# Order edges on TensorE, ScalarE and VectorE, compressed q behind the neighbourhood groups, latent v and k ahead of q, probabilities scaled on VectorE

## The chip, the cores and the metric

The kernel runs on one core of a Trainium2 chip. The metric is device time in microseconds (us), taken from outside the profile. The kernel before takes 1472.89 us, the median of three runs (1472.82 to 1473.05). The kernel multiplies fp32 numbers as pairs of fp32r halves, so TensorE does three products for each one of the reference.

## The reference

One encoder layer on x of 256 tokens by 2048 features, with 256 memory tokens:

```python
h = rmsnorm(x); z = h @ w_in                 # q, k, v (8 heads x 128), c_q (512), c_kv (256), k_rope (64)
A = neighbourhood_attention(q, k, v, rpb)    # softmax(q k' / sqrt(128) + bias) v on a 4 x 64 grid
q2 = rmsnorm(c_q) @ w_uq                     # 8 heads x (128 + 64 rotary)
k2, v2 = split(rmsnorm(c_kv) @ w_ukv)        # 8 heads x (128 + 128)
B = softmax((q2 k2' + rope(q2r) rope(k_rope)') / sqrt(192)) v2
x = x + concat(rmsnorm(A), rmsnorm(B)) @ w_out
x = x + memory_attention(rmsnorm(x), rmsnorm(mem))   # 4 heads of 512
x = x + (silu(n @ w_gate) * (n @ w_up)) @ w_down     # n = rmsnorm(x), d_ff = 5632
out = rmsnorm(x)
```

## The kernel before

**Weights.** All weights stand in one array in the order of their use, as 496 pieces of 128x1024 numbers. SP's queue loads two pieces a transfer into three buffers (`raw`). `split` (L105 to L113) makes two halves of a piece: ScalarE copies it into fp32r (`whi`, L108), then VectorE subtracts that copy (`wlo`, L109). Where a scale is given, the same is L111 on ScalarE and L112 on VectorE. There are three buffers for split pieces, and `piece` (L152) calls for splits two pieces ahead (one ahead for the first 16).

**Products.** `linear` (L225) walks over the 128-row blocks k of a weight and for each does six products of 512 columns on TensorE, three for each half of the tokens (L221 to L223: hi by hi, hi by lo, lo by hi). A full piece is 12 such products. The result gathers in a PSUM buffer `pm` (128x1024); the pool `psm` has two of them. All smaller PSUM tiles (`pt`, `ps`, `py`, `pv`) come from the four buffers of the pool `psa`. A group of latent q or k uses `mm_block` (L186) in place of L221 to L223, and `combine` (L241) adds its two parts: ScalarE copies one (`cmt`, L244), VectorE adds the other (`cmu`, L246). The name of a tile carries a number in the order of the program.

**Background.** Everything beside the products is written as jobs, generators that yield a number of ticks (`Background`, L161). `linear` ticks twice after each k, and a job goes on when its ticks are used up; so the W_ numbers say where in the stream of products the transposes, scores and softmax steps of a head are written. `na_head` (L505) is a head of neighbourhood attention: turn q and k (L303), split, scores, `softmax_steps` (L352: maximum, exponentials, reciprocal, and the scaling of the probabilities on ScalarE at L370), turn the probabilities, values (`head_out`, L498). `compressed` (L464) takes the sums of squares of c_q or c_kv (L253), their rstd (VectorE, POOL, VectorE), evacuates (`ct`, L296), turns it and splits it into `cs`. `rope_job` (L541), `q_job` (L554), `k_job` (L561) and `mla_project` (L567) make latent q, k and the rotary part; `load_mem` (L627) brings the memory's tokens (`mraw`, `mtok`), both in one buffer.

**Order.** Before, the written order is only a priority: a scheduler with a cost model moves an instruction ahead of another on its engine where it holds that to be ready sooner. The projections run as v, c_q, c_kv, four groups q and k of two heads each, the rotary part, q 0, k 0 and 1, q 1, v, then the output projection with the second half of q and k inside it.

```python
        bg.add(rope_job(linear(cs, 4)))
        mla_project(0)
        for i in range(2):
            split_v(linear(cs[:, 4:6], 2), vy_ml[:, 4 * i:4 * i + 4])
```

Of the kernel before, what the change touches and what calls it, by code (L numbers as in the profile page):

```python
# [19 lines left out]
P = 128  # L20
# [31 lines left out]
W_TR = 4  # L52
W_QK, W_EXP, W_PT, W_PV = 4, 3, 5, 6
W_HEADS = 8
W_RS = 5
# [5 lines left out]
def tile_hybrid_encoder(ctx, tc, x, xt, mem, memt, gains, fgain, rope, rpb, weights, out):  # L61
# [9 lines left out]
    psa = ctx.enter_context(tc.tile_pool(name="psa", bufs=4, space=PSUM))  # L71

# [32 lines left out]
    def split(dst_hi, dst_lo, src, scale=None):  # L105

        if scale is None:
            nc.scalar.activation(dst_hi, src, AF.Copy)  # L108
            nc.vector.tensor_sub(dst_lo, src, dst_hi.bitcast(F32))  # L109
        else:  # L110
            nc.scalar.activation(dst_hi, src, AF.Copy, scale=scale)  # L111
            nc.vector.scalar_tensor_tensor(dst_lo, src, scale, dst_hi.bitcast(F32),  # L112
                                           op0=OP.mult, op1=OP.subtract)  # L113
# [72 lines left out]
    def mm_block(ps, whi, wlo, a, first, last):  # L186

        rhs = a.rearrange("p s t -> p (s t)")
        if last and not first:
            nc.tensor.matmul(ps[:, 0:T], wlo, a[:, 0, :], start=False, stop=False)  # L190
            nc.tensor.matmul(ps, whi, rhs, start=False, stop=True)
        else:
            nc.tensor.matmul(ps, whi, rhs, start=first, stop=False)  # L193
            nc.tensor.matmul(ps[:, 0:T], wlo, a[:, 0, :], start=False, stop=last)

    def mm_split(ps, a, b, first, last):

        for i, (u, v) in enumerate(((0, 0), (0, 1), (1, 0))):
            nc.tensor.matmul(ps, a[:, u, :], b[:, v, :], start=first and i == 0, stop=last and i == 2)  # L199
# [18 lines left out]
    def products(o, ak, t, hi, lo, first, last):  # L218

        ts_ = slice(t * P, (t + 1) * P)  # L220
        nc.tensor.matmul(o, ak[:, 0, ts_], hi, start=first, stop=False)  # L221
        nc.tensor.matmul(o, ak[:, 0, ts_], lo, start=False, stop=False)  # L222
        nc.tensor.matmul(o, ak[:, 1, ts_], hi, start=False, stop=last)  # L223

    def linear(a, nk, pm=None, ks=None, cw=CW):  # L225
# [4 lines left out]
        for k in ks or range(nk):  # L230
            if k % per == 0:
# [6 lines left out]
            bg.tick(2)  # L238
        return pm

    def combine(pm):  # L241

        t = scr.tile([P, 2, T], F32, name="cmt", tag="sq")
        nc.scalar.activation(t, pm[:, :, T:2 * T], AF.Copy)  # L244
        dst = scr.tile([P, 2, T], F32, name="cmu", tag="pr", bufs=3)
        nc.vector.tensor_add(dst, pm[:, :, 0:T], t)  # L246
# [3 lines left out]
    def sumsq(dst, src, scale=1.0):  # L250

        junk = scr.tile([P, CW], F32, name="junk", tag="sq")
        nc.scalar.activation(junk[:, :src.shape[-1]], src, AF.Square, scale=scale, accum_out=dst)  # L253

    def square_into(acc, src, first):
        if first:
            nc.scalar.activation(acc, src, AF.Square)
        else:
            q = scr.tile([P, 2, T], F32, name="sq", tag="sq")[:, :src.shape[1]]
            nc.scalar.activation(q, src, AF.Square)  # L260
            nc.gpsimd.tensor_tensor(acc, acc, q, op=OP.add)

    def rstd_of(sums, d, name):

        ms = const.tile([P, TT], F32, name=f"ms_{name}")
        nc.vector.tensor_scalar(ms, sums, 1.0 / d, EPS, op0=OP.mult, op1=OP.add)
# [4 lines left out]
    def rstd_parts(parts, d, name):  # L271

        sums = const.tile([P, TT], F32, name=f"su_{name}")
        nc.vector.tensor_reduce(sums, parts, axis=AX.X, op=OP.add)
        return rstd_of(sums, d, name)

    def rstd_col(acc, n, d, name):

        pc = psa.tile([P, 2 * T], F32, name="pc", tag="a")
        for t in range(TT):  # L280
            for j in range(n):
                nc.tensor.matmul(pc[:, t:t + 1], acc[:, j, t * P:(t + 1) * P], ones[:, 0:1],
                                 start=j == 0, stop=j == n - 1)
# [4 lines left out]
    def rstd_job(acc, n, d, name, wait=1):  # L288
        yield wait
# [3 lines left out]
    def evacuate(pm, dst, rc, w=CW):  # L293

        for t in range(TT):
            nc.scalar.activation(dst[:, t, :], pm[:, t, 0:w], AF.Copy, scale=rc[:, t:t + 1])  # L296

    def turn(src, f0, nf=2):

        pt = psa.tile([P, 2, T], F32, name="pt", tag="a")  # L300
        for f in range(nf):
            for t in range(TT):
                nc.tensor.transpose(pt[:, f, t * P:(t + 1) * P], src[:, t, (f0 + f) * P:(f0 + f + 1) * P], ident)  # L303
# [17 lines left out]
    def residual_job(pm, g, rc=None, parts=None, nxt=None, g0=None, name=None):  # L321


        cs_ = slice(g * CW, (g + 1) * CW)
        for t in range(TT):
            if rc is None:
                nc.vector.tensor_add(xr[:, t, cs_], xr[:, t, cs_], pm[:, t, :])
            else:
                nc.vector.scalar_tensor_tensor(xr[:, t, cs_], pm[:, t, :], rcs[rc][:, t:t + 1], xr[:, t, cs_],
                                               op0=OP.mult, op1=OP.add)  # L330
# [527 lines left out]
```

## Time and profile before

| | us |
|---|---|
| median of three runs | 1472.89 |
| the profiled execution | 1472.88 |
| its span (first to last instruction) | 1471.1 |
| TensorE busy | 1453.7 (99%) |
| VectorE busy | 794.0 (54%) |
| ScalarE busy | 720.1 (49%) |
| GpSimd busy | 22.1 (2%) |

The profiled execution is 1.8 us longer than its span. The HBM traffic is 187 GB/s over the span. The mean granted clock of TensorE is 0.996 of full speed. In the rows, PE is TensorE's products, PEld its weight loads (which run beside products), DVE VectorE, ACT ScalarE, POOL GpSimd and SP the queue that issues transfers. A product's record lasts longer than the distance to the next one's start, since products overlap.

### The profile page before, as it was taken

How to read it: one execution, taken by the hardware profiler on the slowest of the kernel's cores; microseconds unless marked ns; L12 is line 12 of the kernel's file. 1: busy time of each engine (PE TensorE's matmuls, PEld its weight loads, DVE VectorE, ACT ScalarE, POOL GpSimd, SP SyncE). 2: the span in 40 equal slices, each digit the busy share in tenths (PEclk: the TensorE clock that was granted, in tenths of full speed). 3: DMA queues.
4: the chain of work that ended last, by engine and by line, in shares of the span. 5: the costliest groups of instructions: out<-in, count | busy, mean ns of one | idle time of the engine just before them, and what ended most of it. 6: DMA issues, size and time to landing. Idle time of an engine off the chain costs nothing.

```text
span 1471.1 us, 16942 instructions
## 1 busy us (share of the span) xinstructions
PE 1453.7 (99%) x6812; PEld 1212.7 (82%) x6812; DVE 794.0 (54%) x874; ACT 720.1 (49%) x982; POOL 22.1 (2%) x39
## 2 busy tenths in 40 slices
PE   9999999999999999999999999999999999999997
PEld 7878888888888888888888888888888888888886
DVE  5565687667454454545545555445454445555554
ACT  6455677656544554445444444444333444444443
POOL 0000000100000000000000000000000000000000
PEclk9999999999999999999999999999999999999999
DMA  9865444365755444545555555555555555555553
GB/s 356 257 189 172 144 143 144 129 225 198 249 201 172 165 150 166 178 159 184 189 183 199 178 196 195 180 197 180 193 199 198 186 188 194 180 197 193 180 199 115
DMA packets 48718, 275.90 MB, mean 188 GB/s; under 512 B 12992, under 2 KB 13120, under 8 KB 16576
## 3 DMA queue, kind: packets, MB, share of 16 engines
q1 hardware_dynamic: 48064, 273.47, 54.7%
q8 instruction: 53, 0.87, 0.3%
q10 hardware_dynamic: 576, 1.36, 0.3%
q14 instruction: 25, 0.20, 0.0%
HBM read 272.71 MB, written 3.05 MB: 187 GB/s over the span
## 4 chain that ended last, share of the span: by engine, by line
PE 95%; DMA 2%; ACT 1%; DVE 1%; issue 1%; POOL 0%; DVEq 0%; ACTq 0%; POOLq 0%
PE pm L222 28%; PE pm L223 28%; PE pm L221 28%; PE pt L303 2%; PE ps L199 2%; PE py L199 2%; DMA mtok<-in_memt 1%; PE pv L221 1%; PE pv L222 1%; PE pv L223 1%; PE pl L223 0%; PE pl L222 0%; PE pl L221 0%; PE pm L193 0%; ACT whi L108 0%
## 5 line engine op out<-in xcount | busy, mean ns | idle before, releaser
L109 DVE TENSOR_TENSOR wlo<-raw,whi 128x1024 fp32r<-128x1024 f32 (+1 forms) x493 | 602.2, 1223 | 601.9 <-ACT whi L108 601.5
L108 ACT ACTIVATE whi<-raw 128x1024 fp32r<-128x1024 f32 (+1 forms) x493 | 520.8, 1058 | 580.9 <-PE pm L223 565.2
L221 PE MATMUL pm<-whi,x3s 128*128 128x512 f32 x704 | 275.7, 392 | 0.0
L223 PE MATMUL pm<-whi,x3s 128*128 128x512 f32 x704 | 274.1, 389 | 0.0
L222 PE MATMUL pm<-wlo,x3s 128*128 128x512 f32 x704 | 274.0, 389 | 0.0
L223 PEld LDWEIGHTS pm<-whi,x3s 128*128 128x128 f32 x704 | 132.1, 188 | 27.5
L222 PEld LDWEIGHTS pm<-wlo,x3s 128*128 128x128 f32 x704 | 132.2, 188 | 27.0
L221 PEld LDWEIGHTS pm<-whi,x3s 128*128 128x128 f32 x704 | 132.2, 188 | 26.8
L221 PE MATMUL pm<-whi,ms 128*128 128x512 f32 x256 | 101.7, 397 | 0.0
L223 PE MATMUL pm<-whi,ms 128*128 128x512 f32 x256 | 99.9, 390 | 0.0
L222 PE MATMUL pm<-wlo,ms 128*128 128x512 f32 x256 | 99.9, 390 | 0.0
L221 PE MATMUL pm<-whi,ha 128*128 128x512 f32 x224 | 87.5, 391 | 0.0
L223 PE MATMUL pm<-whi,ha 128*128 128x512 f32 x224 | 87.2, 389 | 0.0
L222 PE MATMUL pm<-wlo,ha 128*128 128x512 f32 x224 | 87.2, 389 | 0.0
L221 PE MATMUL pm<-whi,xs 128*128 128x512 f32 (+1 forms) x192 | 74.6, 389 | 0.3 <-ACT whi L108 0.3
L222 PE MATMUL pm<-wlo,xs 128*128 128x512 f32 (+1 forms) x192 | 73.5, 383 | 0.4 <-DVE wlo L109 0.2
L223 PE MATMUL pm<-whi,xs 128*128 128x512 f32 (+1 forms) x192 | 73.2, 381 | 0.0
L223 PEld LDWEIGHTS pm<-whi,ms 128*128 128x128 f32 x256 | 48.1, 188 | 10.4
L222 PEld LDWEIGHTS pm<-wlo,ms 128*128 128x128 f32 x256 | 48.2, 188 | 8.8
L221 PEld LDWEIGHTS pm<-whi,ms 128*128 128x128 f32 x256 | 48.2, 188 | 8.8
L221 PE MATMUL pm<-whi,x2s 128*128 128x512 f32 x128 | 50.1, 391 | 0.8 <-ACT whi L108 0.8
L222 PE MATMUL pm<-wlo,x2s 128*128 128x512 f32 x128 | 49.9, 390 | 0.8 <-DVE wlo L109 0.8
(247 smaller groups left out, 1912.0 us busy)
## 6 DMA issues: line engine op xcount, KB each, us to landing
raw<-in_weights SPq DMA_DIRECT2D x247, 1024.0 KB, 4.9
xr<-in_xt SPq DMA_DIRECT2D x2, 1024.0 KB, 10.7
bias<-skew SPq DMA_DIRECT2D x16, 128.0 KB, 6.4
mraw<-in_mem SPq DMA_DIRECT2D x4, 512.0 KB, 4.8
mtok<-in_memt SPq DMA_DIRECT2D x4, 512.0 KB, 5.1
xf<-in_x SPq DMA_DIRECT2D x7, 256.0 KB, 8.0
fg<-in_fgain SPq DMA_DIRECT2D x1, 1024.0 KB, 7.4
out<-xr SPq DMA_DIRECT2D x2, 512.0 KB, 3.8
```

What stands on the lines that cost most here:

```text
L108: nc.scalar.activation(dst_hi, src, AF.Copy)
L109: nc.vector.tensor_sub(dst_lo, src, dst_hi.bitcast(F32))
L199: nc.tensor.matmul(ps, a[:, u, :], b[:, v, :], start=first and i == 0, stop=last and i == 2)
L221: nc.tensor.matmul(o, ak[:, 0, ts_], hi, start=first, stop=False)
L222: nc.tensor.matmul(o, ak[:, 0, ts_], lo, start=False, stop=False)
L223: nc.tensor.matmul(o, ak[:, 1, ts_], hi, start=False, stop=last)
L303: nc.tensor.transpose(pt[:, f, t * P:(t + 1) * P], src[:, t, (f0 + f) * P:(f0 + f + 1) * P], ident)
```

## The change

Five things change.

1. **Order edges.** `ordered = tc.keep_in_program_order` is put around nearly every instruction of TensorE, ScalarE and VectorE. On each of these engines the instructions then run as they are written. Instructions of POOL and transfers are not wrapped.
2. **Job order and ticks.** Compressed q is projected behind the four neighbourhood groups; compressed kv comes right behind v. The tick numbers change (W_TR, W_QK, W_EXP, W_PT, a W_ROPE of 9, 12 ticks between the two heads of a group), and a narrow k step ticks once.
3. **Latent order.** Behind compressed q come v 0, k 0 and 1, v 1, k 2 and 3, the rotary part, q 0 and q 1; q 2 and q 3 stand in the output projection. The weight array is built in the new order. The jobs of rstd and residual wait until their heads are done.
4. **Scaling.** `softmax_steps` scales the probabilities with VectorE's `tensor_scalar_mul`, not with ScalarE's activation.
5. **Small moves.** The sums of squares of x come one step later; `mtok` has the two buffers of the tag `gate`; the buffer of `qr` lies in another pool.

```diff
--- before.py
+++ after.py
-W_TR = 4
-W_QK, W_EXP, W_PT, W_PV = 4, 3, 5, 6
+W_TR = 5
+W_QK, W_EXP, W_PT, W_PV = 6, 2, 8, 6
 W_HEADS = 8
-W_RS = 5
+W_ROPE = 9
+    ordered = tc.keep_in_program_order
...
         if scale is None:
-            nc.scalar.activation(dst_hi, src, AF.Copy)
-            nc.vector.tensor_sub(dst_lo, src, dst_hi.bitcast(F32))
+            ordered(nc.scalar.activation(dst_hi, src, AF.Copy))
+            ordered(nc.vector.tensor_sub(dst_lo, src, dst_hi.bitcast(F32)))
...
-            bg.tick(2)
+            bg.tick(2 if cw == CW else 1)
...
-    def rstd_job(acc, n, d, name, wait=1):
-        yield wait
+    def rstd_job(acc, n, d, name, ready):
+        while not ready():
+            yield 1
+        yield W_TR
...
         for t in range(TT):
-            nc.scalar.activation(pr[:, t, :], pr[:, t, :], AF.Copy, scale=rs[:, t:t + 1])
+            ordered(nc.vector.tensor_scalar_mul(pr[:, t, :], pr[:, t, :], rs[:, t:t + 1]))
...
-            if j in (5, 6):
+            if j in (6, 7):
...
-        bg.add(compressed(linear(xs, KB), RANK_Q, "q", 0, 4))
         bg.add(compressed(linear(xs, KB, cw=KVR), RANK_KV, "kv", 4, 2))
...
-                bg.add(na_head(2 * i + j, qt, W_TR + (14 if i < NAH // 2 - 1 else 2) * j))
+                bg.add(na_head(2 * i + j, qt, W_TR + 12 * j))
+        bg.add(compressed(linear(xs, KB), RANK_Q, "q", 0, 4))
...
+        def project_v(i):
+            split_v(linear(cs[:, 4:6], 2), vy_ml[:, 4 * i:4 * i + 4])
...
+        project_v(0)
+        project_k(0)
+        project_v(1)
+        project_k(2)
         bg.add(rope_job(linear(cs, 4)))
-        mla_project(0)
-        for i in range(2):
-            split_v(linear(cs[:, 4:6], 2), vy_ml[:, 4 * i:4 * i + 4])
+        project_q(0)
         bg.add(mla_heads())
-        bg.add(rstd_job(acc_na, 1, NAH * P, "na", 2))
+        project_q(1)
+        bg.add(rstd_job(acc_na, 1, NAH * P, "na", lambda: done[G_NA] == NAH))
         for g in range(DM // CW):
             if g == 1:
-                mla_project(2)
-            bg.add(residual_job(linear(vy_na, NAH), g, rc="na"))
+                project_q(2)
+                project_q(3)
+            bg.add(residual_job(linear(vy_na, NAH, ready=lambda: done[G_NA]), g, rc="na"))
...
-                r = hp.tile([P, TT, CW], F32, name="mtok", tag="mraw", bufs=1)
+                r = scr.tile([P, TT, CW], F32, name="mtok", tag="gate")
```

`project_q` and `project_k` are the two halves of `mla_project`, unchanged inside.

**Place A: TensorE, the turn of compressed kv.** `pm_668` gathers c_kv, `ct_880` is its evacuation, `kr_910` its rotary key, `pm_839` the first neighbourhood group. Before, behind c_kv's last products (320 columns):

```order
L221 MATMUL pm_668<-whi_772,xs_78 128x320
L222 MATMUL pm_668<-wlo_773,xs_78 128x320
L223 MATMUL pm_668<-whi_772,xs_78 128x320
L303 MATMUL pt_901<-ident_89,ct_880 128x128 x4
L303 MATMUL pt_939<-ident_89,kr_910 128x128
L221 MATMUL pm_839<-whi_797,xs_78 128x512
L303 MATMUL pt_939<-ident_89,kr_910 128x128
L222 MATMUL pm_839<-wlo_798,xs_78 128x512
L223 MATMUL pm_839<-whi_797,xs_78 128x512
L221 MATMUL pm_839<-whi_797,xs_78 128x512
```

After, `ct_699` is c_kv's evacuation and `pm_654` the first neighbourhood group:

```order
L224 MATMUL pm_654<-whi_683,xs_78 128x512
L225 MATMUL pm_654<-wlo_684,xs_78 128x512
L226 MATMUL pm_654<-whi_683,xs_78 128x512
L309 MATMUL pt_734<-ident_89,ct_699 128x128 x4
L224 MATMUL pm_654<-whi_683,xs_78 128x512
L225 MATMUL pm_654<-wlo_684,xs_78 128x512
L226 MATMUL pm_654<-whi_683,xs_78 128x512
L224 MATMUL pm_654<-whi_683,xs_78 128x512
```

The four transposes of `ct` moved from directly behind c_kv's last product into the middle of the fourth weight piece of the next group, and the rotary key's moved further behind.

**Place B: ScalarE behind v.** `pv_139` to `pv_142` are the sums of v, `vy_na_128` where they go. Before:

```order
L108 ACTIVATE whi_458<-raw_408 128x1024
L108 ACTIVATE whi_478<-raw_456 128x1024
L111 ACTIVATE vy_na_128<-pv_139,rc_x_498 128x4x128
L111 ACTIVATE vy_na_128<-pv_140,rc_x_498 128x4x128
L108 ACTIVATE whi_511<-raw_456 128x1024
L111 ACTIVATE vy_na_128<-pv_141,rc_x_498 128x4x128
L111 ACTIVATE vy_na_128<-pv_142,rc_x_498 128x4x128
L108 ACTIVATE whi_517<-raw_474 128x1024
```

After (`pa_x_143` are the sums of squares of x, in front of v's evacuations):

```order
L257 ACTIVATE junk_492,pa_x_143<-xr_79 128x512
L114 ACTIVATE vy_na_128<-pv_139,rc_x_498 128x4x128
L114 ACTIVATE vy_na_128<-pv_140,rc_x_498 128x4x128
L114 ACTIVATE vy_na_128<-pv_141,rc_x_498 128x4x128
L114 ACTIVATE vy_na_128<-pv_142,rc_x_498 128x4x128
L111 ACTIVATE whi_511<-raw_448 128x1024
L111 ACTIVATE whi_517<-raw_466 128x1024
```

Before, a weight split (`whi_511`) stood between the two pairs of evacuations of v; now all four stand together, and that split behind them.

**Place C: ScalarE and VectorE behind compressed q.** Before, `pm_510` is compressed q, and two weight splits stand between its sums and its evacuations:

```order
L253 ACTIVATE junk_664,ss_q_663<-pm_510,rc_x_498 128x512
L253 ACTIVATE junk_666,ss_q_663<-pm_510,rc_x_498 128x512
L108 ACTIVATE whi_671<-raw_587 128x1024
L296 ACTIVATE ct_713<-pm_510,both_q_687 128x512
L108 ACTIVATE whi_703<-raw_587 128x1024
L296 ACTIVATE ct_713<-pm_510,both_q_687 128x512
L111 ACTIVATE cs_129<-pt_729,gain_80 128x256 x2
L111 ACTIVATE cs_129<-pt_756,gain_80 128x256 x2
```

After, `pm_1522` is compressed q, `pm_1758` the first latent v, `pm_1799` and `pm_1812` the first two halves of latent k, `py_1824` a neighbourhood head's values. ScalarE:

```order
L257 ACTIVATE junk_1752,ss_q_1751<-pm_1522,rc_x_498 128x512
L257 ACTIVATE junk_1754,ss_q_1751<-pm_1522,rc_x_498 128x512
L111 ACTIVATE whi_1761<-raw_1637 128x1024
L111 ACTIVATE pk_1776<-pt_1771 128x2x256
L111 ACTIVATE ml_1756<-pm_1758 128x4x128 x2
L111 ACTIVATE whi_1795<-raw_1637 128x1024
L248 ACTIVATE cmt_1808<-pm_1799 128x512
L302 ACTIVATE ct_1817<-pm_1522,both_q_1785 128x512 x2
L114 ACTIVATE vy_na_128<-py_1824,gain_80 128x256
L264 ACTIVATE sq_1833<-py_1824 128x256
L248 ACTIVATE cmt_1836<-pm_1812 128x512
```

VectorE at the same place:

```order
L112 TENSOR_TENSOR wlo_1762<-raw_1637,whi_1761 128x1024
L112 TENSOR_TENSOR pk_1776<-pt_1771,pk_1776 128x2x256
L270 TENSOR_SCALAR ms_q_1786<-ss_q_1751 128x2
L483 TENSOR_TENSOR both_q_1785<-rc_x_498,rc_q_1788 128x2
L112 TENSOR_TENSOR ml_1756<-pm_1758,ml_1756 128x4x128 x2
L112 TENSOR_TENSOR wlo_1796<-raw_1637,whi_1795 128x1024
L250 TENSOR_TENSOR cmu_1810<-pm_1799,cmt_1808 128x512
L115 SCALAR_TENSOR_TENSOR vy_na_128<-py_1824,gain_80,vy_na_128 128x256
L250 TENSOR_TENSOR cmu_1838<-pm_1812,cmt_1836 128x512
```

Compressed q's evacuation (`ct_1817`) now stands behind the evacuation of the first latent v and behind the copy of the first half of k.

## Rows read from the trace of the kernel before

**Rows 1.** Page, busy us of each engine (share of the span) xinstructions

```profile
PE 1453.7 (99%) x6812; PEld 1212.7 (82%) x6812; DVE 794.0 (54%) x874; ACT 720.1 (49%) x982; POOL 22.1 (2%) x39
```

**Rows 2.** Waits: engine, line, releaser: us in total, times, longest us

```profile
ACT junk L253 <- DMA mtok<-in_memt: 11.6, 4, 4.5
...
PE pt L303 <- ACT ct L296: 2.8, 1, 2.8
PE pt L303 <- ACT s L370: 1.1, 1, 1.1
...
PE pm L193 <- DVE cmu L246: 0.4, 1, 0.4
```

**Rows 3.** Windows: us; PE, PEld, DVE, ACT, POOL busy; clock; DMA; GB/s

```profile
75.00:100.00 25.00, 21.48 (x113) 18.50 (x113) 18.39 (x31) 13.75 (x25) 1.20 (x3) 0.86 0.62 184
200.00:225.00 25.00, 23.32 (x135) 19.56 (x134) 24.14 (x40) 19.46 (x39) 2.08 (x2) 1.00 0.36 120
400.00:425.00 25.00, 23.46 (x102) 18.86 (x102) 11.18 (x11) 11.70 (x15) 1.75 (x1) 1.00 0.65 222
```

**Rows 4.** Timeline, TensorE, 90 to 99: start, us, operation [idle before <-releaser]

```profile
90.66 0.91 PE L303 MATMUL pt<-ident,ct 128*128 128x128 f32 x4 [2.82 <-ACT ct L296]
...
98.08 0.63 PE L221 MATMUL pm<-whi,xs 128*128 128x512 f32 x1
98.51 0.44 PE L222 MATMUL pm<-wlo,xs 128*128 128x512 f32 x1
```

**Rows 5.** Timeline of the start

```profile
4.75 0.63 ACT L108 ACTIVATE whi<-raw 128x512 fp32r<-128x512 f32 x1 [1.59 <-DMA raw<-in_weights]
...
6.14 0.91 ACT L111 ACTIVATE xs<-xf,gain 128x256 fp32r<-128x256 f32 x2 [0.76 <-DMA xf<-in_x]
...
6.70 0.50 PE L221 MATMUL pv<-whi,xs 128*128 128x512 f32 x1 [0.59 <-ACT xs L111]
```

**Rows 6.** Timeline, end of v, 48 to 51

```profile
48.64 1.05 ACT L108 ACTIVATE whi<-raw 128x1024 fp32r<-128x1024 f32 x1
...
50.09 1.37 ACT L111 ACTIVATE vy_na<-pv,rc_x 128x512 fp32r<-128x512 f32 x2 [0.40 <-PE pv L223]
...
50.57 0.39 PE L221 MATMUL pm<-whi,xs 128*128 128x512 f32 x1
50.80 0.39 PE L222 MATMUL pm<-wlo,xs 128*128 128x512 f32 x1
```

**Rows 7.** Groups by line: xcount | busy us, mean ns | idle before, releaser

```profile
L109 DVE TENSOR_TENSOR wlo<-raw,whi 128x1024 fp32r<-128x1024 f32 x491 | 600.8, 1225 | 597.5 <-ACT whi L108 597.0
L108 ACT ACTIVATE whi<-raw 128x1024 fp32r<-128x1024 f32 x491 | 519.7, 1060 | 579.3 <-PE pm L223 565.2 <-PE pv L223 8.6 <-issue 2.4
...
L246 DVE TENSOR_TENSOR cmu<-pm,cmt 128x512 f32<-128x512 f32 x8 | 5.5, 685 | 0.6 <-ACT cmt L244 0.5
...
L244 ACT ACTIVATE cmt<-pm 128x512 f32<-128x512 f32 x8 | 4.8, 599 | 1.6 <-PE pm L191 1.0 <-issue 0.6
```

**Rows 8.** Timeline behind compressed q, 72 to 80

```profile
72.53 0.69 ACT L253 ACTIVATE junk<-pm,rc_x 128x512 f32<-128x512 f32 x1 [1.66 <-PE pm L223]
...
74.01 0.17 DVE L266 TENSOR_SCALAR ms_q<-ss_q 128x2 f32<-128x2 f32 x1 [1.88 <-ACT junk L253]
...
74.99 0.16 DVE L475 TENSOR_TENSOR both_q<-rc_x,rc_q 128x2 f32<-128x2 f32 x1 [0.81 <-POOL rc_q L268]
...
78.75 0.48 DVE L112 SCALAR_TENSOR_TENSOR cs<-pt,gain,cs 128x256 fp32r<-128x256 f32 x1 [0.67 <-ACT cs L111]
...
79.27 0.47 ACT L111 ACTIVATE cs<-pt,gain 128x256 fp32r<-128x256 f32 x1 [0.55 <-DVE cs L112]
```

**Rows 9.** Tiles rt and rotb: count: ns min/median/max, first and last start

```profile
L459 DVE TENSOR_TENSOR rt<-pm,rp x2: 686/689/692, 203.8 to 206.8; 128x512 f32<-128x512 f32 x2
...
L460 DVE TENSOR_TENSOR rotb<-pm,rp x2: 416/416/417, 204.4 to 207.4; 128x256 f32<-128x256 f32 x2
```

**Rows 10.** Groups by line, the scaling of probabilities

```profile
L370 ACT ACTIVATE pr<-pr,rs 128x256 f32<-128x256 f32 x24 | 10.9, 504 | 3.4 <-DVE rs L368 3.4
```

More of the change, by code (lines that the diff above doesn't have):

```diff
@@ L220, in products, with linear @@
         ts_ = slice(t * P, (t + 1) * P)
[L221 to L225, printed above, removed]
+        ordered(nc.tensor.matmul(o, ak[:, 0, ts_], hi, start=first, stop=False))
+        ordered(nc.tensor.matmul(o, ak[:, 0, ts_], lo, start=False, stop=False))
+        ordered(nc.tensor.matmul(o, ak[:, 1, ts_], hi, start=False, stop=last))
+    def linear(a, nk, pm=None, ks=None, cw=CW, ready=None):
         if pm is None:
@@ L230, in linear @@
         for k in ks or range(nk):
+            assert ready is None or ready() > k
             if k % per == 0:
@@ L265, in rstd_of @@
         ms = const.tile([P, TT], F32, name=f"ms_{name}")
[L266 removed]
+        ordered(nc.vector.tensor_scalar(ms, sums, 1.0 / d, EPS, op0=OP.mult, op1=OP.add))
         rc = const.tile([P, TT], F32, name=f"rc_{name}")
@@ L273, in rstd_parts @@
         sums = const.tile([P, TT], F32, name=f"su_{name}")
-        nc.vector.tensor_reduce(sums, parts, axis=AX.X, op=OP.add)
+        ordered(nc.vector.tensor_reduce(sums, parts, axis=AX.X, op=OP.add))
         return rstd_of(sums, d, name)
@@ L324, in residual_job @@
         cs_ = slice(g * CW, (g + 1) * CW)
+        while rc is not None and rc not in rcs:
+            yield 1
         for t in range(TT):
             if rc is None:
-                nc.vector.tensor_add(xr[:, t, cs_], xr[:, t, cs_], pm[:, t, :])
+                ordered(nc.vector.tensor_add(xr[:, t, cs_], xr[:, t, cs_], pm[:, t, :]))
             else:
-                nc.vector.scalar_tensor_tensor(xr[:, t, cs_], pm[:, t, :], rcs[rc][:, t:t + 1], xr[:, t, cs_],
-                                               op0=OP.mult, op1=OP.add)
+                ordered(nc.vector.scalar_tensor_tensor(xr[:, t, cs_], pm[:, t, :], rcs[rc][:, t:t + 1], xr[:, t, cs_],
+                                               op0=OP.mult, op1=OP.add))
         if nxt is not None:
@@ L382, in tile_hybrid_encoder @@
     for _ in range(N_WARM):
-        nc.tensor.matmul(idle[:, 0:P], ones, ones, start=True, stop=True)
+        ordered(nc.tensor.matmul(idle[:, 0:P], ones, ones, start=True, stop=True))
     with ExitStack() as at:
@@ L519, in na_head, with rope_job @@
             head_out(vy_na, h, acc_na, G_NA, got[0])
+        qrs = {}
+        def rope_job(pm):
+            rt = scr.tile([P, TT, CW], F32, name="rt", tag="ev")
+            for t in range(TT):
+                v, d = (a[:, t, :].rearrange("p (h c) -> p h c", c=ROPE) for a in (pm, rt))
+                rotate(d, v, t, MLH)
+            yield W_ROPE
+            for f in range(0, 4, 2):
+                pt = turn(rt, f)
+                qr = ap.tile([P, 2, 2, T], F32R, name="qr", tag="qr", bufs=2)
+                split(qr[:, :, 0, :], qr[:, :, 1, :], pt)
+                qrs[f], qrs[f + 1] = qr[:, 0], qr[:, 1]
+                yield 2
         for i in range(NAH // 2):
@@ L539, in mlp @@
             return pools[0]
-        def rope_job(pm):
-            rt = scr.tile([P, TT, CW], F32, name="rt", tag="ev")
-            for t in range(TT):
-                v, d = (a[:, t, :].rearrange("p (h c) -> p h c", c=ROPE) for a in (pm, rt))
-                rotate(d, v, t, MLH)
-            yield W_TR
-            for f in range(0, 4, 2):
-                pt = turn(rt, f)
-                qr = mlp().tile([P, 2, 2, T], F32R, name="qr", tag="qr", bufs=2)
-                split(qr[:, :, 0, :], qr[:, :, 1, :], pt)
-                qrs[f], qrs[f + 1] = qr[:, 0], qr[:, 1]
-                yield 2
         def q_job(pair, pm):
@@ L578, in mla_project @@
                 bg.add(k_job(pair + i, pm))
-            bg.add(q_job(pair + 1, linear_fm(cs, 4)))
+        def project_v(i):
+            split_v(linear(cs[:, 4:6], 2), vy_ml[:, 4 * i:4 * i + 4])
         def mla_head(h):
@@ L615, in tile_hybrid_encoder @@
     for g in range(DM // CW):
-        bg.add(residual_job(linear(vy_ml, MLH), g, "ml", p2, x2s, G_XQ, "x2"))
+        bg.add(residual_job(linear(vy_ml, MLH, ready=lambda: done[G_ML]), g, "ml", p2, x2s, G_XQ, "x2"))
     with ExitStack() as at:
```

105 lines of the change are left out of this document (54 added, 51 removed).

## The prediction

> **What bounds the kernel now.** I read the busy times first, then the list of TensorE's waits, then the table of windows, then the timeline wherever a window was not full. TensorE is busy for 1453.7 of 1471.1 us [rows 1], so an edit can win only idle TensorE time, or time at a lower clock, and it loses whatever makes TensorE wait anew. Three windows are not full before the end [rows 3]: 75 to 100 us (21.48 of 25 us busy, granted clock 0.86), 200 to 225 (23.32) and 400 to 425 (23.46). The waits name the causes [rows 2]: transposes that wait for an evacuation of the compressed kv (2.8 us), transposes that wait for a softmax's scaling (1.1), and a matmul group that waits 0.4 us until VectorE has read the PSUM buffer that it wants. From about 460 us to the tail the windows were full, so I look for changes only in the first third.
>
> **What the change removes.** In the program of before, the four kv transposes stand right behind the last product of compressed kv, whose sums, rstd and evacuation are not done. They start at 90.66 after 2.82 us of idle time, 3.0 us later than full speed would have it, and from there to 98.51 TensorE runs at the lower of its two levels [rows 4]. In these 7.85 us it does six transposes and 13 products of 512 columns. At full speed a product starts every 0.227 us [rows 6], so this is 13 x 0.227 + 0.6 = 3.6 us of work, and 4.2 us are lost. Place one costs 7.2 us. In the new order those transposes stand in the middle of a weight piece, three and a half pieces into the first neighbourhood group; a piece is 12 products, 2.7 us. For compressed q the chain took 2.6 us from the first sum to both_q [rows 8], and two evacuations of 0.69 follow: some 4 us, with over 9 us of products beside it. This loss goes, and nothing is late in its place.
>
> Place two, 200 to 225: 25 - 23.32 = 1.7 us visibly idle. A product's record is 0.39 us long while the next starts after 0.227, so each visible gap hides another 0.16 us; with four of them 2.4 us. The heads 6 and 7, which crowded there, are now 12 ticks apart. I count it as gone, and price what replaces it below. Place three, 400 to 425: two gaps, 1.54 us visible, 1.9 with the hidden part. ScalarE sat up to 4.5 us in front of sums of squares on token tiles of the memory that had not landed [rows 2], with weight splits behind them. The tile now has two buffers of its own, and its first two transfers are issued some 50 weight pieces before they are used. It goes. Removed: 7.2 + 2.4 + 1.9 = 11.5 us.
>
> **What it adds, in order of time.** Fixed orders are followed instruction by instruction; what a wait holds up is all that stands behind it on its engine.
>
> At the start ScalarE now makes the two xs halves before the first weight half. It did the weight at 4.75, while x was still on its way, and the xs pair at 6.14 for 0.91 us; the first product came at 6.70 [rows 5]. Now: 6.14 + 0.91 + 0.63 for the weight half = 7.7; the second product needs VectorE's half, 0.69 us more, 8.4 instead of 7.0. Price 1.4 us. Bounds: 0.7, if the first landing comes earlier, and 4, if the 1.6 us pause brings the lower clock.
>
> Between v and compressed kv, ScalarE has four evacuations of v (1.37 us a pair) before it may split the second kv piece; before, that split ran at 48.64, 1.9 us ahead of the last v product's end at 50.57 [rows 6]. Call that end zero. The last pair starts then, ends at 1.4 to 1.9 (the first pair waits for sums that now come two pieces later), the split ends at 2.9, VectorE's half at 4.2. The first kv piece lasts 18 products of 320 columns, 2.6 us. The pause is 4.2 - 2.8 = 1.4 us; bounds 0.5 and 3.5.
>
> The large term is where latent v and k now follow compressed q. There are two wide PSUM buffers (pm). Compressed q keeps one until its evacuation ct, which is written behind the first half of k; so v, the halves of k and v again go through the other one. Durations [rows 7]: weight split 1.06 on ScalarE and 1.23 on VectorE, 512-wide reads of PSUM 0.60 and 0.69; back to back each is about 0.09 shorter, a hand-over costs 0.05. The 256-wide halves of cs are 0.47 and 0.48, and ScalarE's second waits for VectorE's first [rows 8]. Zero is now compressed q's last product.
> - First half of k. TensorE has v and a group of transposes, 3.2 us. The buffer is free once both token halves of v are split. ScalarE: two sums 1.3, weight split to 2.2. VectorE: weight 3.4, pk 4.1, then ms_q, POOL and both_q, 1.15 as in [rows 8], 5.25; then v low 5.9, high 6.5, low 7.3. Wait 4.1 us.
> - Second half of k takes the buffer of the first: cmt 0.60, cmu 0.69, two hand-overs, 1.4 us.
> - Fourth k group, counted from head 7's value product: two 256-wide halves, a square, cmt and a weight split on ScalarE (0.47 + 0.48 + 0.39 + 0.60 + 0.96 = 2.9), VectorE's weight half 1.23, then seven halves that take turns (0.65, 0.45, 0.47, 0.60, 0.69, 0.60, 0.69 with v's second piece), 8.3, with sixteen hand-overs 9.1. TensorE has v, transposes and a k half, 2.7 + 0.45 + 1.4 = 4.55. Wait 4.5 us.
> - The rotary product waits 0.3 us for a cmu. The second q group needs the buffer that the rotation reads: VectorE is 0.5 us late and reads PSUM with six operations of 0.69 and 0.42 [rows 9], some 3.4 us, against 2.8 us of the first q group. Wait 1.1 us.
>
> Sum 4.1 + 1.4 + 4.5 + 0.3 + 1.1 = 11.4 us. Two of these pauses are longer than the 2.82 us after which the lower clock was seen [rows 4], so I expect that clock twice; a whole such stretch cost 4.2 us. Much of one is hidden, since ScalarE and VectorE are the later ones there, so I take one price: 15.6 us. Bounds: 8 (half a wait less at each place, no lower clock) and 20 (both stretches in full). The trace of before shows a wait for a PSUM buffer of only 0.4 us [rows 2], because there the rotary and q groups, with other heads' work between them, took turns with the k groups.
>
> The Trainium skill's page "Perfetto Trace Analysis" (Optimizing Tensor Performance, Matmuls) has a rule that speaks against this order: independent matmul groups should rotate through different PSUM banks, so that evacuating one overlaps the products of the next. As an estimate by that rule alone, six groups through one buffer would each pay their evacuation, 6 x 1.4 = 8.4 us, without the queues that I count; no run here shows it so far, and the 0.4 us is the only trace of it.
>
> The scaling that moves to VectorE takes two ScalarE steps of 0.50 us off each head [rows 10]; on VectorE it costs between 0.16 (a 128x2 operation) and 0.48 us each, the 256-wide one of [rows 8], and I take 0.4. Its cover: from a neighbourhood head's scores to its transposes lie 10 ticks, five steps of six products, 6.8 us, and mask and reduce (0.69 each, as the wide row of VectorE in [rows 7]), two exponentials (0.50, as the scaling), a reciprocal (0.16) and two scalings add up to 0.69 + 0.69 + 1.0 + 0.16 + 0.8 = 3.3, with hand-overs about 4. Without that cover it would be 2 x 0.4 us a head, 16 us in all for 20 heads. The other new waits of jobs, and the marks that fix an order that was already there, I count as nothing under the same products.
>
> **Sum.** -11.5 + 1.4 + 1.4 + 15.6 = +6.9 us. The profiled execution took 1472.88 us, 1.8 more than its span, and the median of the runs is 1472.89, so the sum may stand on either: 1479.8, which I round down to 1479, since missed overlaps tend to shorten such chains.
>
> **Rivals.**
> 1. Faster. TensorE's waits at latent v and k are covered, because VectorE and ScalarE are as far ahead as before. For it: VectorE is busy 54% in all [rows 1], and the same evacuations cost only 2.4 us at 200 us. Against it: the buffer's release stands in a written order that I can count. The point that decides is whether VectorE's second half of v is done 3.2 us after compressed q. Then -11.5 + 1.4 + 1.4 + 2.4 = -6.3: 1466.5.
> 2. No difference. The waits are there, but stay at their lower bound, with no lower clock: -11.5 + 2.8 + 8 = -0.7: 1472.2, and up to 1475.6 with the full 11.4. For it: the pauses of 1.1 us at 213 left the clock at 1.00 [rows 2, 3]. Against it: 2.82 us did not.
> 3. Much slower. The clock drops at the start and twice at latent k: -11.5 + 4 + 3.5 + 20 = +16: 1489.
> 4. The order is not what decides: the removed waits come back elsewhere, since a fixed order lets nothing ready pass. It would show as many small waits in the cross-attention, some +3 to +6 us on top of rival 2, 1477, near the forecast with another cause.
>
> **How the numbers follow.** Forecast 0.52 (its own range 1475.5 to 1486), rival 1 0.14, rival 2 0.20, rival 3 0.07, rival 4 0.07. A measurement of this kernel can tell 0.2%, 2.9 us, from no change: below 1470.0 is faster, above 1475.8 slower. Rival 1 is faster; rival 2 lies within but for a few hundredths on either side; the others are slower: 0.16, 0.18, 0.66. The range 1468.5 to 1486 leaves out most of rival 1 and of rival 3.
>
> **What would show it.** Right: at the first group of latent k TensorE waits about 4 us for VectorE's ml, the second half waits 1.4 us for cmu, the fourth again over 3 us for ml, and the windows there show a granted clock under 1; windows near 90 and 400 are full; the first product stands at 7.7. Wrong: waits on ml under 2 us in all, or a clock of 1.00 through it (rival 2), or waits spread over the cross-attention (rival 4). A time under 1470 would say that I counted queues that ran ahead.

## The result and the profile after

The changed kernel takes 1483.53 us, the median of four runs (1483.34 to 1485.05), against 1472.86 us for the kernel before in the same runs: 10.67 us more, a ratio of 1.0076 (95% interval 1.0059 to 1.0094). It is slower, as forecast, inside the forecast's own range (1475.5 to 1486), and by 4 us more than the 6.9 us of the sum. The profiled execution is 1483.61 us long, its span 1481.8 us.

The busy times, against [rows 1]:

```profile
PE 1457.5 (98%) x6812; PEld 1216.9 (82%) x6812; DVE 810.6 (55%) x914; ACT 705.7 (48%) x942; POOL 21.2 (1%) x39
```

For the same 6812 instructions TensorE is busy 3.8 us longer: more of them ran at the lower clock than before. The list of TensorE's waits, against [rows 2], is a new list:

```profile
PE pm L196 <- DVE ml L112: 8.2, 2, 4.3
PE pm L196 <- DVE cmu L250: 1.5, 1, 1.5
PE pv L224 <- ACT whi L111: 1.3, 1, 1.3
...
PE pm L225 <- DVE wlo L112: 0.8, 1, 0.8
PE pm L196 <- ACT cmt L248: 0.7, 1, 0.7
PE pt L309 <- POOL kr L493: 0.4, 1, 0.4
PE pv L225 <- DVE wlo L112: 0.2, 1, 0.2
PE pm L224 <- ACT whi L111: 0.2, 1, 0.2
```

The transposes' waits for `ct` and for the softmax are gone, and L196, a group of latent k or q, waits for VectorE's `ml` (the evacuation of latent v) 8.2 us in two pieces. The windows of [rows 3], and the first 25 us (us; PE, PEld, DVE, ACT, POOL busy; clock; DMA; GB/s):

```profile
0.00:25.00 25.00, 22.40 (x90) 18.74 (x91) 12.51 (x19) 13.72 (x21) 2.66 (x13) 0.93 0.93 341
50.00:75.00 25.00, 23.96 (x139) 21.83 (x138) 14.28 (x18) 15.47 (x28) 1.41 (x2) 1.00 0.74 225
75.00:100.00 25.00, 24.64 (x114) 20.15 (x113) 18.05 (x26) 12.56 (x16) 1.44 (x2) 1.00 1.02 240
200.00:225.00 25.00, 15.29 (x59) 12.42 (x58) 12.82 (x19) 11.08 (x20) 1.44 (x2) 0.72 0.24 83
225.00:250.00 25.00, 24.29 (x120) 20.28 (x120) 20.48 (x32) 13.93 (x22) 0.70 (x1) 0.94 0.43 147
400.00:425.00 25.00, 25.00 (x112) 20.67 (x112) 14.20 (x17) 14.41 (x21) 0.00 (x0) 1.00 0.61 204
```

The kernel before at the start:

```profile
0.00:25.00 25.00, 23.36 (x102) 19.49 (x103) 14.44 (x22) 15.12 (x22) 2.66 (x13) 1.00 0.91 343
```

Place three is full and place one is but for 0.36 us, both at a clock of 1.00. Place two has become the worst stretch of the program: TensorE is busy for 15.29 of 25 us at a clock of 0.72. And the start did 90 products instead of 102: 12 x 0.227 = 2.7 us are lost in the first 25 us, part of them by the clock (0.93). The 1.04 us missing from 50 to 75 us are the pause behind v.

The chain that ended last, from compressed q's sums to the first half of latent k (its longest pieces: start, us, what):

```profile
197.43 1.45 ACT junk L257 x4
198.88 0.95 ACT whi L111
199.86 1.23 DVE wlo L112
201.09 0.60 DVE pk L112
201.84 0.71 POOL rc_q L272
202.73 0.61 DVE ml L112
203.37 0.60 ACT ml L111
204.00 0.70 DVE ml L112
204.84 0.76 PE pm L196
```

This is the queue of the prediction, step by step: ScalarE's sums and weight split, VectorE's weight half and `pk`, then both_q, which waits for POOL, and only behind it the two halves of `ml` that free the PSUM buffer. Until 208.33 compressed q's own buffer is held too.

The start (start, us, operation), against [rows 5]: x landed at much the same time, but the weight half stands behind it on ScalarE.

```profile
5.95 0.91 ACT L114 ACTIVATE xs<-xf,gain 128x256 fp32r<-128x256 f32 x2 [2.79 <-DMA xf<-in_x]
...
6.76 2.08 ACT L111 ACTIVATE whi<-raw 128x512 fp32r<-128x512 f32 x3
...
7.43 0.49 PE L224 MATMUL pv<-whi,xs 128*128 128x512 f32 x1 [1.32 <-ACT whi L111]
...
8.15 0.50 PE L225 MATMUL pv<-wlo,xs 128*128 128x512 f32 x1 [0.23 <-DVE wlo L112]
```

Behind v, against [rows 6], ScalarE makes four evacuations in a row, after a wait for POOL's rstd of x, and the weight splits follow:

```profile
52.76 2.42 ACT L114 ACTIVATE vy_na<-pv,rc_x 128x512 fp32r<-128x512 f32 x4 [1.29 <-POOL rc_x L272]
...
55.05 2.97 ACT L111 ACTIVATE whi<-raw 128x1024 fp32r<-128x1024 f32 x3
...
57.44 0.41 PE L225 MATMUL pm<-wlo,xs 128*128 128x320 f32 x1 [0.85 <-DVE wlo L112]
```

The scaling takes 0.35 us on VectorE, against 0.50 on ScalarE in [rows 10]:

```profile
L378 DVE TENSOR_SCALAR pr<-pr,rs 128x256 f32<-128x256 f32 x24 | 7.4, 351 | 0.4
```

### The profile page after: what moved, and what is told of

It reads as the page before. It is cut to its first block, busy times and chain, and to the rows that moved or that the text cites. A ratio compares the mean times of both kernels' runs of the same rounds, so it can differ in the third digit from the quotient of the medians.

```text
span 1481.8 us, 16942 instructions
## 1 busy us (share of the span) xinstructions
PE 1457.5 (98%) x6812; PEld 1216.9 (82%) x6812; DVE 810.6 (55%) x914; ACT 705.7 (48%) x942; POOL 21.2 (1%) x39
## 4 chain that ended last, share of the span: by engine, by line
PE 96%; DVE 1%; ACT 1%; issue 1%; DMA 0%; POOL 0%; DVEq 0%; POOLq 0%; ACTq 0%
PE pm L224 28%; PE pm L225 28%; PE pm L226 28%; PE pt L309 3%; PE ps L202 2%; PE py L202 2%; PE pv L225 1%; PE pv L226 1%; PE pv L224 1%; PE pm L196 1%; PE pl L225 0%; PE pl L224 0%; PE pl L226 0%; DMA xf<-in_x 0%; PE pm L194 0%
## 5 line engine op out<-in xcount | busy, mean ns | idle before, releaser
L224 PE MATMUL pm<-whi,x2s 128*128 128x512 f32 x128 | 50.0, 390 | 0.0
L226 PE MATMUL pm<-whi,x2s 128*128 128x512 f32 x128 | 49.8, 389 | 0.0
```

What stands on the lines that cost most here:

```text
L224: ordered(nc.tensor.matmul(o, ak[:, 0, ts_], hi, start=first, stop=False))
L226: ordered(nc.tensor.matmul(o, ak[:, 1, ts_], hi, start=False, stop=last))
```

## The experiments

Theory A: a fixed order lets a PSUM buffer and a weight split stand behind work that is not ready, so the cost lies in what is written next to what. Theory B: ScalarE and VectorE have more to do around latent q, k and v than TensorE's products give them time for, whatever the order. Each time below is the difference to the kernel before in the same batch of runs; the intervals are 1.2 to 2.1 us wide to either side. The changed kernel itself is +10.7 us, with 2.6 us to either side.

| kernel | us | to before | ratio, 95% interval |
|---|---|---|---|
| e1_ct_early | 1475.12 | +2.7 | 1.0012 to 1.0029 |
| e2_fill | 1478.52 | +6.1 | 1.0029 to 1.0054 |
| e3_start_v | 1478.52 | +6.1 | 1.0029 to 1.0056 |
| e4_act_scale | 1481.26 | +9.3 | 1.0052 to 1.0080 |
| e5_no_edges | 1471.12 | -1.3 | 0.9976 to 0.9994 |
| e6_cq_earlier | 1475.45 | +3.4 | 1.0018 to 1.0035 |
| e7_three_edges | 1472.43 | +0.4 | 0.9997 to 1.0014 |
| e8_spread | 1472.48 | +0.5 | 0.9994 to 1.0012 |
| e9_pe_edges | 1472.99 | +0.5 | 0.9994 to 1.0012 |
| e10_before_pe | 1474.52 | +2.0 | 1.0004 to 1.0022 |
| e11_before_mtok | 1470.62 | -1.9 | 0.9977 to 0.9994 |
| e12_edges_part | 1467.00 | -4.8 | 0.9955 to 0.9980 |

**e1: compressed q evacuated at once.**

```diff
-            yield W_EV
+            if name == "kv":
+                yield W_EV
             both = const.tile([P, TT], F32, name=f"both_{name}")
...
-            yield W_EV
+            yield W_EV if name == "kv" else 1
             ct = scr.tile([P, TT, CW], F32, name="ct", tag="ev")
```

> The changed kernel with one edit: compressed q's rstd is written right behind its sums, and its evacuation one tick later, ahead of the evacuation of the first latent v. Theory A (the written order holds the PSUM buffers): the first half of latent k gets compressed q's buffer about 4.0 us after its last product instead of 7.8, so its wait falls from 4.30 us to about 1; the second half waits about 1.2, the fourth about 1.5 instead of 3.94, no wait passes 2 us, and the clock stays at 1.00. Of the 16.8 us lost from 200 to 240 us some 5 are left: about 1472 us, 1469 to 1476. Theory B (ScalarE and VectorE have more to do there than TensorE gives time for, in whatever order): the waits change places and their sum stays within 3 us of 10.4: 1480 to 1485 us.

It gave 8.0 us back (10.7 to 2.7) where A said 11.5 and B at most 3.5. Its waits:

```profile
PE pm L196 <- DVE ml L112: 5.4, 2, 4.4
PE pv L224 <- ACT whi L111: 3.3, 1, 3.3
...
PE pm L196 <- ACT ct L302: 1.0, 1, 1.0
```

The first half of k waits 1.0 us for `ct` and the second 1.0 us for `ml`, as A had it. The fourth still waits 4.4 us, and the clock is 0.86 from 200 to 225 us where A said 1.00: I had overlooked that a pair of `cs`, the evacuations of compressed q's transposes, still stands in front of latent v's on ScalarE and VectorE. (In this execution x landed a microsecond later, hence 3.3 us at the start.)

**e2: the same waits filled with products that nothing reads** (16, 4, 0 and 14 in front of the four halves of latent k).

```diff
+                    for _ in range(n):
+                        ordered(nc.tensor.matmul(fl, hi[:, 0:P], cs[:, 4].rearrange("p s t -> p (s t)"),
+                                                 start=True, stop=True))
                 pm = psm.tile([P, 2, 2 * T], F32, name="pm", tag="pm")
```

> The changed kernel with products that nothing reads (16, 4 and 14 of 512 columns, 3.6, 0.9 and 3.2 us at full speed) in front of the first, second and fourth half of latent k, where TensorE waited 4.30, 1.54 and 3.94 us. Theory A: the waits stay as long, but TensorE is not idle in them, so the granted clock stays near 1.00 from 200 to 240 us and the 6.4 us that were lost there beside the waits (16.8 less 10.4) come back for the most part: 1477 to 1480 us. Rival: the lost 6.4 us are not the clock's but the cost of waits that I did not count: no gain, 1483 us or more.

4.6 us came back by adding work. The stretch of this kernel, and then of the changed one, in windows:

```profile
200.00:210.00 10.00, 8.77 (x45) 6.91 (x44) 4.85 (x8) 3.92 (x7) 0.70 (x1) 1.00 0.52 193
210.00:220.00 10.00, 8.80 (x45) 7.12 (x44) 6.72 (x10) 6.69 (x12) 0.74 (x1) 1.00 0.01 3
220.00:230.00 10.00, 9.60 (x48) 7.70 (x46) 9.16 (x16) 5.75 (x9) 0.00 (x0) 1.00 0.48 162
```

```profile
200.00:210.00 10.00, 4.22 (x13) 2.92 (x12) 5.13 (x8) 4.20 (x7) 0.70 (x1) 0.70 0.49 183
210.00:220.00 10.00, 8.47 (x38) 7.07 (x36) 4.27 (x7) 4.70 (x9) 0.74 (x1) 0.79 0.04 15
220.00:230.00 10.00, 7.59 (x26) 6.48 (x27) 7.20 (x11) 5.63 (x11) 0.00 (x0) 0.66 0.31 105
```

The clock is 1.00 in place of 0.70, 0.79 and 0.66: the lower clock behind the waits cost about 4.6 us by the medians, 5.6 by the two profiled executions (1478.02 against 1483.61). The waits themselves are not shorter; most of their time is spent on useless products, and 3.2 us are left.

**e3: the start and v as the scheduler had them.**

```diff
                 split(hi[:, d], lo[:, d], raw[:, c])
+                if p == 0 and c is cuts[0]:
+                    split_x(0)
...
             split_v(pv[i], vy_na[:, 4 * i:4 * i + 4], rx)
+            if i == 0:
+                wt.split()
```

> The changed kernel with two places of the order put back: at the start ScalarE and VectorE split the first weight half ahead of x's first blocks, and behind v the split of the second compressed kv piece stands between the two pairs of v's evacuations. Theory A: the first product comes at 6.7 instead of 7.43 with no wait for a lower half behind it (2.7 us with the lower clock that followed), and the 1.5 us pause behind v goes: 4.2 us less, about 1479.3 us, 1478 to 1481. Rival: the time comes back at the next transfer or split, since weights arrive at the same pace: less than 1 us gained, above 1482.5 us.

4.6 us came back, where 4.2 were expected; the first 25 us now hold 101 products at a clock of 1.00, v's last product starts at 50.59 us instead of 52.97, and of the 1.04 us behind v 0.15 are left. The time was not lost again later. But in the profiled execution the clock at latent k was higher too (0.80 and 1.00 in the two windows from 200 to 250 us, against 0.72 and 0.94), so the 4.6 us need not be the price of the two places alone.

**e4: scaling on ScalarE again.**

```diff
-            ordered(nc.vector.tensor_scalar_mul(pr[:, t, :], pr[:, t, :], rs[:, t:t + 1]))
+            ordered(nc.scalar.activation(pr[:, t, :], pr[:, t, :], AF.Copy, scale=rs[:, t:t + 1]))
```

> The changed kernel with the probabilities scaled on ScalarE again (two steps of 0.50 us a head there, two of 0.35 us less on VectorE); all else stays. Theory A: from a head's scores to its transposes TensorE has 6.8 us of products and the chain needs about 4, so either engine is hidden: 1483.5 us, 1481.5 to 1485.5. Rival (the scaling is on the path, as in the 1.1 us wait of before): slower by some 1 us a crowded head, 1487 us or more, or faster by as much if VectorE is the later one.

9.3 against 10.7 us, intervals that overlap: not told apart from no difference. (1481.26 lies 0.2 us under the range that Theory A gave.) The scaling is not the cause of the loss.

**e5: the changed kernel without edges.**

```diff
-    ordered = tc.keep_in_program_order
+    ordered = lambda i: i
```

> The changed kernel without the order edges: job order, ticks, scaling and all else stay, and the scheduler may move instructions. It then splits the first weight half ahead of x, splits a weight between the two pairs of v's evacuations, and evacuates compressed q's first half ahead of latent v, its second half one weight split later. Theory A (the written order, not the new job order, costs the time): the start and v give back 4.2 us, and the waits at latent k shrink to some 2.5 + 1 + 2 us with little lower clock, 16.8 to about 8: 1470 us, 1466 to 1475. Rival (the new job order costs it whatever the edges): 1478 us or more.

12.0 us less, and a little faster than before. With job order, ticks and scaling unchanged, it is the edges that cost, and Theory B alone can't be the cause: ScalarE and VectorE have the same work here. e9 below, which keeps the edges on TensorE and is 10.2 us faster than the changed kernel all the same, puts the cost on those of ScalarE and VectorE. Latent k still waits once for `ml` (2.4 us), and TensorE is 1.8 us idle near 94 us, at a clock of 0.94, for a weight split that ScalarE starts behind its evacuations of transposes (`qk`), though the first of these weights landed at 91.3 us:

```profile
94.28 2.94 ACT L111 ACTIVATE whi<-raw 128x1024 fp32r<-128x1024 f32 x3
95.38 0.49 PE L224 MATMUL pm<-whi,xs 128*128 128x512 f32 x1 [1.04 <-ACT whi L111]
```

```profile
75.00:100.00 25.00, 23.19 (x103) 18.75 (x102) 15.09 (x18) 10.78 (x15) 0.00 (x0) 0.94 0.81 203
```

**e6, e7, e8: compressed q ahead of the fourth group; with e3's edits; with half of latent v and k in the output projection.**

```diff
         for i in range(NAH // 2):
+            if i == NAH // 2 - 1:
+                bg.add(compressed(linear(xs, KB), RANK_Q, "q", 0, 4))
             pm = linear(xs, KB)
```

The weight array follows the same order.

> The changed kernel with compressed q projected ahead of the fourth neighbourhood group instead of behind it; all else stays. Theory A (compressed q's PSUM buffer, held until an evacuation that stands late in the written order, makes the waits): the buffer is free when latent k begins, the first half waits under 0.5 us; the second and the fourth still wait for latent v's evacuation, 1.5 and 2 to 3 us. Of the 16.8 us some 5 are left: 1471.5 us, 1468 to 1476. Theory B (the engines have more to do there than there is time for): heads 6 and 7 now crowd the same place as in before, so the waits are as long or longer: 1483 us or more.

> Compressed q ahead of the fourth group, and the first weight half ahead of x and a weight split between the two pairs of v's evacuations, together. Theory A: the three prices add up, 1483.5 - 12 - 4.2 = 1467.3 us, 1464 to 1471, faster than before. Rival: they share one cause, and the two small places are hidden behind the large one: no less than the kernel with compressed q alone, 1471 us.

```diff
         project_k(0)
-        project_v(1)
-        project_k(2)
...
             if g == 1:
+                project_v(1)
+                project_k(2)
                 project_q(2)
```

> As the one before, and the second latent v and the third and fourth half of k stand in the output projection with q 2 and q 3 (head 7 comes 8 ticks behind head 6 instead of 12). Theory A: no half of k stands directly behind another short group that is not evacuated but the second, so the fourth half's wait goes, 2 to 3 us more: 1465 us, 1462 to 1469. Rival: the second half of latent v and k meets the residual sums in the output projection, whose long groups hold a PSUM buffer, and waits there: 1467 us or more.

e6 won 7.2 us of 12. The long wait is gone, and others stand there:

```profile
PE pm L196 <- DVE ml L112: 3.8, 2, 2.7
PE pm L224 <- DVE cmu L250: 3.6, 3, 1.6
...
PE pm L196 <- DVE rotb L469: 1.3, 1, 1.3
```

These 8.7 us are six waits, each of a group for the evacuation of the one but one before it. That may be of B's kind in part, since heads 6 and 7 now lie beside the latent groups; no run separates it. Of the changed kernel's 10.4 us of waits there (4.30, 1.47, 3.94 and 0.71) only 1.7 are gone: what e6 won is for the most part the clock, which stands at 1.00 from 200 to 250 us in place of 0.72 and 0.94. e7 added the 3.0 us of the other two edits (4.2 expected) and only reached the kernel before. In e8 the waits behind the moved groups went along with them (2.31 and 1.05 us at 242 to 246 us), and the clock of that window, 225 to 250 us, fell to 0.86; nothing was won. e6 came in at the edge of its range and e7 and e8 outside theirs, since I held compressed q's buffer for the cause of nearly all of the loss at latent k, 12 us; with the group moved, 7.2 came back.

**e9: edges on TensorE alone; e10: the kernel before with edges on TensorE and two buffers for `mtok`.** The first diff is e9's (on TensorE's instructions `ordered` becomes `pe_ordered`), the second e10's.

```diff
-    ordered = tc.keep_in_program_order
+    pe_ordered = tc.keep_in_program_order
+    ordered = lambda i: i
```

```diff
+    ordered = tc.keep_in_program_order
...
-        nc.tensor.matmul(o, ak[:, 0, ts_], hi, start=first, stop=False)
+        ordered(nc.tensor.matmul(o, ak[:, 0, ts_], hi, start=first, stop=False))
```

> The changed kernel with order edges on TensorE alone; ScalarE and VectorE are left to the scheduler. Theory A (the edges on ScalarE and VectorE cost the time, that on TensorE saves it): the start, v and the release of compressed q's buffer stand as without any edges, and the 4.0 us that the kernel without edges lost near 94 us, where its scheduler had put scores in front of a weight piece's products, do not come: some 4 us under that kernel, 1467 us, 1464 to 1470. Rival (the edges pay only together, since the scheduler's order on one engine assumes its own order on the others): more and longer waits than without edges, 1472 us or more.

> The kernel before with two edits: order edges on TensorE, and two buffers for the memory's tokens; job order, ticks and scaling on ScalarE as before. Theory A: the turn of compressed kv stands three weight pieces later and no longer waits (7.2 us by the prediction), and the wait for the token tiles near 403 us goes (1.9 us); the rest stays: 1472.3 - 9.1 = 1463 us, 1460 to 1467. Rival: the scheduler had moved those transposes since nothing better was ready, so the wait returns on another instruction: 1469 us or more.

Both fell to their rivals: no gain over e5, and 2.0 us slower than before. (e10 holds e11's edit, which wins 1.9 us by itself, so its edges cost some 3.9.) The 1.8 us that e5 lost near 94 us were at most in part due to scores, which e9's expectation blamed: with TensorE's order fixed 1.0 us of waits for the same weight split is left there. In e10 the transposes stand three pieces later, as wanted, and TensorE waits in the same place for something else. Its ScalarE, then its TensorE:

```profile
88.25 0.47 ACT L254 ACTIVATE junk<-pm,rc_x 128x256 f32<-128x256 f32 x1 [4.04 <-PE pm L224]
...
90.51 0.84 ACT L297 ACTIVATE ct<-pm,both_kv 128x256 f32<-128x256 f32 x2 [0.83 <-DVE both_kv L476]
91.23 2.95 ACT L109 ACTIVATE whi<-raw 128x1024 fp32r<-128x1024 f32 x3
```

```profile
92.34 0.80 PE L222 MATMUL pm<-whi,xs 128*128 128x512 f32 x1 [4.13 <-ACT whi L109]
```

ScalarE sat idle for 4.04 us in front of compressed kv's sums, with three weight splits behind them; the weights of the first two had landed at 85.64 us, halfway through. In the kernel before it sat as long in the same place (4.04 us, up to 87.87), with weights that had landed at 85.40.

**e11: two buffers for `mtok` alone**, in the kernel before.

```diff
-                r = hp.tile([P, TT, CW], F32, name="mtok", tag="mraw", bufs=1)
+                r = scr.tile([P, TT, CW], F32, name="mtok", tag="gate")
```

> The kernel before with two buffers for the memory's tokens and nothing else. Theory A: ScalarE no longer stands in front of a transfer with weight splits behind it; the two waits near 403 us go and 1.9 us with them, about 0.13%: 1470.5 us. Rival: TensorE is held there by something else, or the transfers, now side by side with the weights', take as long: within 0.5 us of before.

1.9 us less, as expected; the window from 400 to 425 us is full.

**e12: e11, and edges on the three engines from compressed kv to the last neighbourhood group alone.**

```diff
+    def ordered(i):
+        return tc.keep_in_program_order(i) if fixed[0] else i
...
+        fixed[0] = True
         bg.add(compressed(linear(xs, KB, cw=KVR), RANK_KV, "kv", 4, 2))
...
+        fixed[0] = False
         ml = xsp.tile([P, KB, 2, T], F32R, name="ml", tag="xsA")
```

> The kernel before (its job order, ticks and scaling) with two buffers for the memory's tokens, and with order edges on TensorE, ScalarE and VectorE from compressed kv to the end of the fourth neighbourhood group alone; the start, v and latent q, k and v stay with the scheduler. Theory A (the loss at 90 us is ScalarE's evacuation of compressed kv that the scheduler put in front of weight splits, so it takes an edge on ScalarE to remove it, and edges cost only where short groups follow each other): the stretch from 80 to 100 us is full, 200 to 225 us as before: 1470.6 - 7.2 = 1463.4 us, 1461 to 1467, faster than both kernels. Rival (edges on that stretch make as many new waits as they remove): 1469 us or more.

1467.00 us, 0.33% under the kernel before and faster than the changed one by 15.5 us: the best version here, at the upper end of its range. Windows of it:

```profile
75.00:100.00 25.00, 24.19 (x139) 21.50 (x138) 18.63 (x26) 15.14 (x25) 1.39 (x2) 1.00 0.85 265
...
200.00:225.00 25.00, 23.34 (x136) 19.61 (x135) 23.92 (x39) 19.02 (x38) 2.33 (x3) 1.00 0.32 113
```

Place one is busy for 24.19 us at a clock of 1.00, where before had 21.48 at 0.86 [rows 3], and place two is as before. Over e11 that is 2.9 us by the medians of two batches and 4.0 by the profiled spans (1465.1 against 1469.1), not the 7.2 expected: the transposes of the rotary key now wait 1.5 us for POOL at 100 us, and three new waits at 78 and 89 us take 0.8 us together.

## Why the prediction was right, and where its sizes were off

- **The waits at latent k** were the main term, and they came where and for what the prediction said: 4.30 us forecast as 4.1, 1.47 as 1.4, 3.94 as 4.5; 0.7 for the 1.1 of the second q group; the 0.3 of the rotary product did not come. Sum 10.4 against 11.4. Theory A holds for them: without edges 12.0 us go (e5, which also frees the start and v), with edges on TensorE alone nearly as much (e9), and with an earlier evacuation 8.0 (e1).
- **The lower clock** behind them is a term that was mis-sized: one price of 4.2 us was taken, since much of a second was held to be hidden. Two stretches came, and in them TensorE is busy for 7.95 and 5.50 us at a granted clock of 0.50, the lower of its levels:

```profile
204.02:214.26 10.24, 7.95 (x25) 6.60 (x26) 2.89 (x4) 3.12 (x5) 0.00 (x0) 0.50 0.30 104
221.08:227.91 6.83, 5.50 (x17) 4.76 (x18) 4.21 (x7) 4.33 (x8) 0.00 (x0) 0.50 0.44 151
```

There a product of 512 columns starts 0.43 us after the one before it (213.21, 213.64, 214.07), at full clock 0.23 (214.39, 214.62). So some 6.3 of these 13.4 us are the clock's, an estimate from these rows; e2's medians say about 4.6, its profiled execution 5.6. With the waits that makes 16.7 us, against 15.6. By the same estimate the stretch of the kernel before, with 6.39 us busy at that clock from 91.77 to 98.60, lost 3.0 us and not 4.2, since two waits of 0.29 and 0.25 us lie inside it. So the price of one stretch was too high and the count one too low, and by luck these errors partly cancel.
- The rule of the Trainium skill's page "Perfetto Trace Analysis" (Optimizing Tensor Performance, Matmuls), that independent groups should rotate through PSUM banks, gave 8.4 us. The trace agrees in kind, with 10.4 us of waits for the release of PSUM buffers, but e1 shows that rotation alone doesn't decide: with the same two buffers the first wait fell from 4.30 to 1.0 us by an evacuation written earlier.
- **The start** is the other mis-sized term: 1.4 us forecast, 2.7 measured (v's last product starts 2.6 us later, at 52.97 instead of 50.35). The first product came at 7.43, earlier than the 7.7 forecast; what I left out of the value, though not of its bound of 4, is the clock, 0.93 in the first 25 us where it was 1.00.
- **v to compressed kv**: 1.4 us forecast; 1.04 visible in the two waits, 1.4 with the hidden part of a 320-column product. e3 gave back this and the start, 4.6 us against 2.7 + 1.4, with some help of the clock at latent k, as said there.
- **What was removed**: the losses at places one and three are gone in the profile after. The 1.9 us of place three are shown by e11. Of place one's 7.2 us, 0.4 are left in the changed kernel, where the rotary transposes wait for POOL; in the order of the kernel before e12 wins only 2.9 to 4.0 there, since other waits come up. Its cause was half seen. I read it as transposes that stood too early. e10 shows that moving these alone wins nothing, because ScalarE's queue, with the weight splits behind compressed kv's sums, makes the same wait. e12, with edges on all three engines over that stretch, removes it; an edge on ScalarE alone was not run, so that it is ScalarE's is argued, not shown. (In the new job order without edges, e5, the same window still loses 1.8 us of waits, at a clock of 0.94.)
- **The scaling** at nothing: e4 shows no difference that could be told.

The sum with measured terms is -11.1 + 2.7 + 1.4 + 16.7 = +9.7. TensorE's last product starts 9.8 us later than before (1471.53 against 1461.72). From that product's end to the end of the span it is 9.9 us instead of 9.0, in the output's transfer, which the change does not touch. Together that is the 10.7 us. It closes for the two profiled executions; with e2's 4.6 in place of 6.3 some 1.7 us stay open, which is within the noise of that difference. Against the 6.9 us of the forecast's sum, the clock, the start and the transfer cost 4.3 us more, and the waits and place one 0.6 less.

Of the rivals, the first (VectorE and ScalarE far enough ahead) and the second (no lower clock) are refuted by the windows. The third put the start's bound and both stretches in full, and the truth lies between it and the forecast. The fourth, small waits spread over the cross-attention, is not in the trace: the list of TensorE's waits has none behind 236 us.

## What to carry to other kernels

In this kernel a fixed order paid where long groups follow each other and the scheduler had put an instruction that waits in front of weight splits (e12, 2.9 us over e11), and cost where short groups share two PSUM buffers, at the start and behind v (12.0 us came back without the edges, e5). So fix the order stage by stage, and not everywhere. With an order fixed, write the evacuation that frees a buffer early (e1), and a weight split in front of an instruction that waits for the last product (e3, behind v). Before moving a waiting instruction, look at what the other engines' queues hold at that moment: the same wait may stand there under another name, as in e10.

## What was not expected of the hardware

Products that nothing reads, put into waits, made the kernel 4.6 us faster, with the granted clock at 1.00; e2's expectation forecast that, once the waits had been measured. And a pause's length did not by itself tell whether the clock falls: before, 2.82 us of idle time led to 0.86 in its window, and in e9 a wait of 2.42 us at latent k to 0.85 from 195 to 205 us, while in the profiled execution of e6 one of 2.73 us left it at 1.00. It differs between executions of one kernel too: the mean clock of e6's lay between 0.995 and 0.998.
